# Zero-padded lo keys: both score products of a grouped head on 128 rows

## The chip, the core and the metric

The kernel runs on one core of a Trainium2 chip. Its engines are TensorE (PE, whose weight loads the profile lists as PEld), VectorE (DVE), ScalarE (ACT), GpSimd (POOL) and SyncE (SP, which issues most DMAs). Each engine works through its own list of instructions in order and waits on semaphores that the others raise. The metric is the device time of one execution in microseconds (us); lower is better.

## The reference

Two layers of a hybrid transformer trunk run over 128 context tokens and 512 latent tokens with shared weights. The part that matters here is the grouped-query attention of the latent tokens: 8 query heads of 64 channels share 2 key/value heads, and each latent query sees 640 keys (512 latent, 128 cached).

```python
def _gqa_attend(q, k, v):
    ...
    scale = HEAD_DIM ** -0.5

    def one(qblk):
        s = jnp.einsum('bqhgd,bkhd->bhgqk', qblk, k).astype(jnp.float32) * scale
        p = jax.nn.softmax(s, axis=-1).astype(v.dtype)
        return jnp.einsum('bhgqk,bkhd->bqhgd', p, v)
```

Beside it run a gated linear recurrence (RG-LRU) and a differential attention with 4 heads of two components of 32 channels. An output projection and a gated convolutional feed-forward network follow in each layer.

## The kernel before

All products are split for precision: a float32 value is the sum of a rounded hi part and a lo part (its remainder), and hi·hi, hi·lo and lo·hi are accumulated. The weights stream from DRAM, ACT rounds them (L329) and DVE subtracts (L330).

A layer has five stages: the input projections, during whose last part the context's attention runs; the attention of the latent tokens; the output projection; the two groups of the feed-forward network; residuals and norms in between. The order in which the instructions of one engine stand is written at build time. In the projections `Flow` writes side work when its due time has come. In the attention `Plan` places tasks by assumed lengths, keys and limited room (three pairs of PSUM banks `ps`, for example). A grouped score task is entered there with 540 ns.

**Queries.** For query head h of key/value head g the stationary tile `qa` has 128 rows: rows 64g to 64g+63 hold the hi part of the 64 channels, the other 64 rows the lo part (L828 to L848).

**Keys.** `k_stack` (L867) makes three transposes for 128 keys. Two go to `kk`, which has for each key/value head the hi part in both halves of the 128 rows. The third has the lo parts of both heads one above the other, and one ACT copy (L885) puts it into `kl`, a tile of 128 rows x 640 columns in the pool `tslots` (11 slots).

**Scores.** The unit G of the attention is one query head with one tile of 128 queries; there are 32 of them per layer. Its scores are 128 x 640 and lie in two PSUM banks of 320 columns. Each bank takes two products: `kk` against all 128 rows of `qa` (L1144), then `kl` against the 64 rows that hold the query's hi part (L1145):

```python
pe.matmul(s[:, b * 512:b * 512 + CH], lhsT=Q[:, qs], rhs=kk[:, ks], start=True, stop=False)
pe.matmul(s[:, b * 512:b * 512 + CH], lhsT=Q[hr, qs], rhs=kl[hr, ks], start=False, stop=True)
```

Then DVE takes the row maximum (L1155), ACT the exponential (L1159), which frees the pair of banks, DVE the reciprocal of the sum (L1164), POOL scales the probabilities (L1170), PE transposes them (L1179) into another pair of banks, ACT copies them out (L1184), and PE multiplies them with the values (L1202). The unit D of the differential heads (16 per layer) has two scores of one 96-row product per bank (L1149). PE also does 8 products per row block of the conditioning weights (L487, `ada`) between the units.

**The slots around it.** The pool `halves` has 22 slots of 128 rows x 1292 columns. Activations `hh` and `hl`, `cx` (the context's queries and keys), `kk`, the RG-LRU tiles and `mix` (the attention's input to the output projection) lie in it. A tile that takes over a slot waits for the last reader of the tile that was there. `mix_out` (L637) is the end of the RG-LRU: ACT copies the hi part (L639), DVE subtracts the lo part (L640).

Of the kernel before, what the change touches and what calls it, by code (L numbers as in the profile page):

```python
# [22 lines left out]
T = L + S  # L23
# [27 lines left out]
def f32(ap):  # L51
    return ap.bitcast(F32)


class Flow:
    """Order in which the program is written down. The tensor engine's products are the clock: after each block of
    them step() writes the side work that is due by then, as far as the vector engine's time allows."""
# [36 lines left out]
class Plan:  # L94
    """Order in which the attention is written down: tasks with an engine, a length, what they wait for and what they
    hold, started in the order of their keys as engines come free."""
# [49 lines left out]
def plan_attention(plan, par, ngen, unit, values, stack, ada, split, ready):  # L146
    """the tasks of a layer's attention: lengths in ns, what they wait for, and keys by the place of their unit"""
# [65 lines left out]
def hybrid_kernel(ctx: ExitStack, tc: tile.TileContext, i, o):  # L213
# [27 lines left out]
    def psum_mode(double, single):  # L241
        """the accumulators as so many pairs of banks and so many single banks"""
        psum.close()
        for key, n in (("ps", double), ("pb", single)):
            if n:
                mode[key] = psum.enter_context(tc.tile_pool(name=key, bufs=n, space=bass.MemoryType.PSUM))
# [9 lines left out]
    def pb2(name, cut=CH):  # L256
        """two banks for all tokens and where they are cut"""
        return [pb(name), pb(name), cut]
# [77 lines left out]
    def weights(ahead=2):  # L336
        """the next 128 rows x 1024 of weights in two float32r parts; the one after it is split now"""
        done = lambda: sum(isinstance(z, tuple) for z in split_done)
        while done() < ahead and pos[1] < len(parts) and len(split_done) - done() < 2:
            split_next()  # L340
        return split_done.pop(0)
# [9 lines left out]
    def pow_rstd(ss, n, mean):  # L351
        """(ss * mean + eps) ** -0.5 on [128, n]"""
        a = small("rs_a", n)
        r = small("rs_r", n)
        pool.tensor_scalar(out=a, in0=ss, scalar1=mean, scalar2=EPS, op0=ALU.mult, op1=ALU.add)
        pool.tensor_tensor(out=r, in0=a, in1=mhalf[:, 0:n], op=ALU.pow)
        return r

# [5 lines left out]
    # norm1_g and the bias of the first shift and scale, as rows  # L364
# [50 lines left out]
    def late_constants():  # L415
# [3 lines left out]
        # ffn convolution weights and biases as columns  # L419
# [14 lines left out]
        # differential-attention lambda, on every partition  # L434
# [6 lines left out]
        # softplus(-lambda) = max(-lambda, 0) + 2 atanh(z / (2 + z)), z = exp(-|lambda|), and the factors of log a  # L441
# [35 lines left out]
    res = {}  # L477

    def ada_gen(l, u):
        """one third of the modulation of a layer: a row block of its weights each time"""  # L480
        acc = pb("ada")
        for k in range(KD):
            while not split_done:
                split_next()
            n = split_done.pop(0)
            for j in range(4):
                pe.matmul(acc[32 * j:32 * j + 32, :], lhsT=cc[:, k].rearrange("p a b -> p (a b)"), rhs=raws[n][:, j, :],  # L487
                          start=(k == 0), stop=(k == KD - 1), tile_position=(0, 32 * j))
            load_to(n + 2)
            if k == KD - 2:  # L490
                bias, ar, src = tslot("abias", 512), tslot("arow", 512), i["ada_b"]
                sp.dma_start(out=bias, in_=bass.AP(tensor=src.tensor, offset=src.offset + l * 6 * D + u * 2048,
                                                   ap=[[512, 4], [0, 32], [1, 512]]))
            fl.now += 1100
            yield
        dve.tensor_tensor(out=ar, in0=acc, in1=bias, op=ALU.add)
        if u:
            d = drp.tile([2, 1024], F32, tag=f"gate{u}", name=f"gate{u}")
            for j in range(2):
                r = 32 * (j + (0 if u == 1 else 2))  # L500
                sp.dma_start(out=d[:, j * 512:(j + 1) * 512], in_=ar[r:r + 2, :])
            res["g", l, u] = d
        yield
        pt = pb("adaT")
        for b in range(4):
            pe.transpose(pt[:, b * 128:b * 128 + 128], ar[:, b * 128:b * 128 + 128], ident)
        c = smp.tile([128, 2, 4, 4], F32, tag=f"cm{u}", bufs=2, name=f"cm{u}")
        for r in range(2):
            dve.tensor_copy(out=c[:, r], in_=pt.rearrange("p (b j q) -> p q j b", b=4, j=4)[:, r])
        res["c", l, u] = c.rearrange("p r j b -> p r (j b)")  # L510
# [8 lines left out]
    def mod_cols(c_sh, c_sc, gain, name):  # L519
        """A = (1 + sc) * g, B = sh as columns [128, cond, 8]"""  # L520
        a = smp.tile([128, 2, KD], F32, tag=name, bufs=2, name=name)
        for r in range(2):
            dve.scalar_tensor_tensor(out=a[:, r], in0=c_sc[:, r], scalar=1.0, in1=gain, op0=ALU.add, op1=ALU.mult)
        return a, c_sh

# [12 lines left out]
    def norm_a(t):  # L538
        """a token tile by its rstd"""
        r = row_rstd(t)  # L540
        n = [tslot("xn", 512) for _ in range(2)]
        for hf in range(2):
            pool.tensor_scalar(out=n[hf], in0=x[:, t, hf * 512:hf * 512 + 512], scalar1=r, scalar2=0.0, op0=ALU.mult, op1=ALU.add)
        return n
# [46 lines left out]
    def stat_mm(acc, w, hh, hl, c, n0=0, n1=KD):  # L591
        """rows of weights stationary, one half of the tokens moving"""
# [9 lines left out]
    def tok_acc(name):  # L602
        """accumulators of 512 columns for the five token tiles"""
        box = {}

        def get(t):
            if t not in box:
                box[t] = pb(name)
            return box[t]
        return get  # L610

# [16 lines left out]
    def mixer(l, hh, hl, first=None):  # L628
# [119 lines left out]
        # stationary / moving stacks of the attention and what they come from  # L748
# [33 lines left out]
        def rope(src, t, tab, nh, hd):  # L782
            """src * cos + swapped(src) * sin on [128, nh * hd], in place"""
# [83 lines left out]
        def k_stack(kf, c0):  # L867
            """kf [128 tok, 2 heads of 64] float32 -> columns c0.. of kk (hi; hi) and of the lo of both heads"""
# [10 lines left out]
            def tr():  # L879
# [5 lines left out]
                act.activation(out=kkq[1][:, c0:c0 + 128], in_=f32(pt[:, 256:384]), func=ACTF.Copy)  # L885
# [6 lines left out]
        def d_stack(df, dest, c0, order, jp):  # L892
            """df [128 tok, 4 comps of 32] -> stacks of 96 rows, in columns c0.. of dest (two comps each): four steps"""
# [42 lines left out]
        def values():  # L936
            kkq.extend([v2(half("kk", F32R), T), tslot("kl", T, F32R)])
# [83 lines left out]
        def ctx_probs(qT, kT, kd):  # L1021
            """softmax numerators of 4 context score blocks and their sums; row tiles write to different banks"""
# [103 lines left out]
        dn, mixf, PTs = [], {}, {}  # L1126

        def unit(kind, h, q):
            """scores, softmax and transposed probabilities of one tile of queries of one head"""
# [4 lines left out]
            def score(c):  # L1134
# [3 lines left out]
                if kind == "G":  # L1138
                    kv = h // 4
                    Q, hr = qa[p][:, e], slice(64 * kv, 64 * kv + 64)  # L1140
                    kk, kl = kkq[0][:, kv], kkq[1]
                    for b in range(2):
                        ks = slice(b * CH, b * CH + CH)
                        pe.matmul(s[:, b * 512:b * 512 + CH], lhsT=Q[:, qs], rhs=kk[:, ks], start=True, stop=False)  # L1144
                        pe.matmul(s[:, b * 512:b * 512 + CH], lhsT=Q[hr, qs], rhs=kl[hr, ks], start=False, stop=True)  # L1145
# [43 lines left out]
        def values_of(kind, p, q):  # L1189
            """values of a pair of heads for one tile of queries, and of the context's with the last"""  # L1190
# [97 lines left out]
    def tok_products(nk, stat, done, last=4):  # L1288
        """one half of the columns: token tiles stationary, weights moving; the last row blocks go tile by tile"""
# [26 lines left out]
    def norm_pipe(t, AB, h):  # L1316
        """norm of token tile t as side work; transposes wait until their input is there"""
# [167 lines left out]
    # silu of the conditioning vectors as columns, replicated over 32 stationary columns  # L1485
# [158 lines left out]
```

## Time and profile before

| | |
|---|---|
| median of 3 runs | 1685.59 us (1685.24 to 1686.19) |
| span of the profiled execution | 1688.6 us; no time outside the span is given |
| PE busy | 1649.6 us, 98% of the span |
| DVE, ACT, POOL busy | 943.9, 725.1, 341.2 us (56%, 43%, 20%) |
| attention of the latent tokens, layer 0 and 1 | from 175.7 to 328 us and from 1004.7 to 1151 us of the span |

An engine's busy time counts its own instructions, and idle time before an instruction is put down to what ended it. PE's products are pipelined, so the time that a product costs is the distance between the starts of two products, not the duration in its row. [...]

### The profile page before, as it was taken

The numbers are of one execution on the slowest core, as the hardware profiler recorded it, in microseconds if no ns is written. First come the engines' busy times: TensorE is split into PE (matmuls) and PEld (weight loads), VectorE is DVE, ScalarE is ACT, GpSimd is POOL, SyncE is SP. The second block draws the span as 40 slices with busy tenths as digits, with TensorE's granted clock in tenths as the row PEclk, the third lists the DMA queues.
The fourth block names the chain that finished last, engine by engine and source line by source line (L and its number), as shares of the span: only waits on it lengthen the run. The fifth ranks groups of instructions, "written<-read, shape, count | busy, mean of one in ns | idle before, by whom it ended". The sixth has DMA issues, their size and how long they took to land. (4 is left out here: it accounts for less than half of the span.)

```text
span 1688.6 us, 25351 instructions
## 1 busy us (share of the span) xinstructions
PE 1649.6 (98%) x10070; PEld 1409.1 (83%) x10070; DVE 943.9 (56%) x1548; ACT 725.1 (43%) x1490; POOL 341.2 (20%) x742
## 2 busy tenths in 40 slices
PE   6999999999999999999999999999999999999998
PEld 4778666689999889999887776667899998899986
DVE  5787666466555334555377775665645553345544
ACT  4745566744333212333247455675433331133331
POOL 4162232213111000111053412320411110011101
PEclk9999799999999999999999998999999999999999
DMA  9222355521222321222212213343121322121212
GB/s 332 75 68 82 125 177 182 186 75 51 76 76 74 127 75 50 75 77 77 98 42 76 63 57 125 108 151 130 39 88 50 100 100 75 50 100 51 100 63 87
DMA packets 99434, 161.03 MB, mean 95 GB/s; under 512 B 10670, under 2 KB 69222, under 8 KB 94196
## 3 DMA queue, kind: packets, MB, share of 16 engines
q1 hardware_dynamic: 98068, 158.00, 27.7%
q8 instruction: 79, 1.29, 0.3%
q0 software_dynamic: 1040, 1.14, 0.2%
q14 instruction: 39, 0.32, 0.1%
q10 hardware_dynamic: 208, 0.28, 0.0%
HBM read 155.95 MB, written 3.44 MB: 94 GB/s over the span
## 5 line engine op out<-in xcount | busy, mean ns | idle before, releaser
L330 DVE TENSOR_TENSOR wl<-raw,wh 128x1024 fp32r<-128x1024 f32 x180 | 220.2, 1229 | 408.8 <-ACT wh L329 407.9
L345 PE MATMUL uacc<-hl,wh 128*128 128x320 f32 (+2 forms) x1408 | 436.1, 310 | 0.8 <-DVE hl L574 0.5
L344 PE MATMUL uacc<-hh,wh 128*128 128x320 f32 (+2 forms) x1408 | 436.6, 310 | 0.0
L346 PE MATMUL uacc<-hh,wl 128*128 128x320 f32 (+2 forms) x1408 | 436.4, 310 | 0.1
L329 ACT ACTIVATE wh<-raw 128x1024 fp32r<-128x1024 f32 x180 | 189.6, 1059 | 179.0 <-PE tacc L346 143.0
L345 PEld LDWEIGHTS uacc<-hl,wh 128*128 128x128 f32 x1408 | 265.0, 188 | 1.7 <-DVE hl L574 1.6
L346 PEld LDWEIGHTS uacc<-hh,wl 128*128 128x128 f32 x1408 | 265.7, 189 | 0.7 <-DVE wl L330 0.7
L344 PEld LDWEIGHTS uacc<-hh,wh 128*128 128x128 f32 x1408 | 264.8, 188 | 0.3
L344 PE MATMUL tacc<-wh,g 128*128 128x512 f32 x440 | 173.9, 395 | 0.0
L345 PE MATMUL tacc<-wl,g 128*128 128x512 f32 x440 | 173.5, 394 | 0.0
L346 PE MATMUL tacc<-wh,g 128*128 128x512 f32 x440 | 173.5, 394 | 0.0
L1155 DVE TENSOR_REDUCE nm<-S 128x1 f32<-128x640 f32 x128 | 104.0, 821 | 75.9 <-PE S L1145 53.7
L1159 ACT ACTIVATE P<-S,nm 128x640 f32<-128x640 f32 x128 | 101.3, 793 | 57.3 <-DVE nm L1155 46.6
L1362 POOL TENSOR_SCALAR ca<-u,fcol 128x642 f32<-128x642 f32 x44 | 39.1, 889 | 417.2 <-issue 244.0
L1170 POOL TENSOR_SCALAR P<-P,den 128x640 f32<-128x640 f32 x96 | 79.2, 828 | 216.7 <-DVE den L1164 130.5
L1358 ACT ACTIVATE u<-uacc 128x192 f32<-128x192 f32 (+1 forms) x88 | 29.1, 331 | 185.3 <-PE uacc L346 185.3
L346 PEld LDWEIGHTS tacc<-wh,g 128*128 128x128 f32 x440 | 82.6, 188 | 19.7
L345 PEld LDWEIGHTS tacc<-wl,g 128*128 128x128 f32 x440 | 82.7, 188 | 19.2
L344 PEld LDWEIGHTS tacc<-wh,g 128*128 128x128 f32 x440 | 82.6, 188 | 19.3
L344 PE MATMUL acc<-wh,hh 128*128 128x512 f32 x240 | 97.7, 407 | 0.0
L345 PE MATMUL acc<-wl,hh 128*128 128x512 f32 x240 | 95.9, 400 | 0.0
L346 PE MATMUL acc<-wh,hl 128*128 128x512 f32 x240 | 95.6, 398 | 0.0
(290 smaller groups left out, 2703.2 us busy)
## 6 DMA issues: line engine op xcount, KB each, us to landing
raw<-in_ffn_w_up_dram SPq DMA_DIRECT2D x44, 1024.0 KB, 4.9
raw<-in_ada_w_dram SPq DMA_DIRECT2D x40, 1024.0 KB, 4.9
raw<-in_ffn_w_down_dram SPq DMA_DIRECT2D x20, 1024.0 KB, 5.0
raw<-in_w_in_dram SPq DMA_DIRECT2D x16, 1024.0 KB, 8.6
araw<-in_ada_w_dram SPq DMA_DIRECT2D x16, 512.0 KB, 10.1
raw<-in_w_out_dram SPq DMA_DIRECT2D x8, 1024.0 KB, 5.0
gates<-gate SPq DMA_DIRECT2D x8, 512.0 KB
x<-in_x_sample_dram SPq DMA_DIRECT2D x4, 512.0 KB
```

The lines of the kernel that those rows point to most:

```text
L329: act.activation(out=wh, in_=raw, func=ACTF.Copy)
L330: dve.tensor_tensor(out=wl, in0=raw, in1=f32(wh), op=ALU.subtract)
L344: pe.matmul(out, lhsT=lh, rhs=rh, start=start, stop=False)
L345: pe.matmul(out, lhsT=lh, rhs=rl, start=False, stop=False)
L346: pe.matmul(out, lhsT=ll, rhs=rh, start=False, stop=stop)
L1155: dve.tensor_reduce(out=box["nm", c], in_=view(c), op=ALU.max, axis=AX.XY, negate=True)
L1159: act.activation(out=box["P"][c].rearrange("p (a b) -> p a b", a=2), in_=view(c), func=ACTF.Exp, bias=box["nm", c], accum_out=box["den"][: ...
L1170: pool.tensor_scalar(out=P[-1], in0=P[-1], scalar1=den[:, 1 + comps:2 + comps], scalar2=0.0, op0=ALU.mult, op1=ALU.add)
L1358: act.activation(out=u[:, 1 + cut:1 + L], in_=acc[1][:, 0:L - cut], func=ACTF.Copy)
L1362: pool.tensor_scalar(out=out, in0=u[:, 1:1 + n], scalar1=wcol(1), scalar2=wcol(3), op0=ALU.mult, op1=ALU.add)
```

## The change

The lo keys move from one 640-column tile in `tslots` to a tile in `halves` with one block of 640 columns for each key/value head. In the block of head g only rows 64g to 64g+63 hold lo keys; POOL sets the other 64 rows to zero once per layer (the tile is not written there again). The ACT copy of 128 rows becomes two copies of 64 rows. The second score product uses all 128 rows of `qa`, of which the lo rows now meet zeros. Apart from this only comments differ.

```diff
@@ k_stack
-                act.activation(out=kkq[1][:, c0:c0 + 128], in_=f32(pt[:, 256:384]), func=ACTF.Copy)
+                for g in range(2):
+                    gs = slice(64 * g, 64 * g + 64)
+                    act.activation(out=kkq[1][gs, g, c0:c0 + 128], in_=f32(pt[gs, 256:384]), func=ACTF.Copy)
@@ values
-            kkq.extend([v2(half("kk", F32R), T), tslot("kl", T, F32R)])
+            kkq.extend([v2(half("kk", F32R), T), v2(half("kl", F32R), T)])
+            for g in range(2):
+                pool.memset(f32(kkq[1][64 - 64 * g:128 - 64 * g, g]), 0.0)
@@ unit, score
-                    Q, hr = qa[p][:, e], slice(64 * kv, 64 * kv + 64)
-                    kk, kl = kkq[0][:, kv], kkq[1]
+                    Q, kk, kl = qa[p][:, e], kkq[0][:, kv], kkq[1][:, kv]
...
-                        pe.matmul(s[:, b * 512:b * 512 + CH], lhsT=Q[hr, qs], rhs=kl[hr, ks], start=False, stop=True)
+                        pe.matmul(s[:, b * 512:b * 512 + CH], lhsT=Q[:, qs], rhs=kl[:, ks], start=False, stop=True)
```

PE, DVE and SP keep their instructions in the same order. ACT has ten more (five per layer). Before, around the last key block of layer 0 (`cdk` and `cx` belong to the context, `kk` and `kl` are the keys):

```order
114 L1008 ACTIVATE cdk<-acc 128x256
115 L883 ACTIVATE kk<-kT 128x2x128
116 L885 ACTIVATE kl<-kT 128x128
117 L1016 ACTIVATE cx<-cdkT 128x256
118 L329 ACTIVATE wh<-raw 128x1024
```

The same place of ACT with the change:

```order
114 L1012 ACTIVATE cdk<-acc 128x256
115 L883 ACTIVATE kk<-kT 128x2x128
116 L887 ACTIVATE kl<-kT 64x128 x2
117 L1020 ACTIVATE cx<-cdkT 128x256
118 L329 ACTIVATE wh<-raw 128x1024
```

One copy has become two of half the rows, and nothing else has moved. POOL gets its two memsets between the sum of the RG-LRU's directions (`lruS`) and the norm of the first key tile (`rs_a`, `rs_r`), here in layer 0:

```order
60 L356 TENSOR_TENSOR rs_r<-rs_a,mhalf 128x8
61 L734 TENSOR_TENSOR lruS<-lruI 128x640
62 L941 MEMSET kl 64x640 x2
63 L355 TENSOR_SCALAR rs_a<-hss 128x2
64 L356 TENSOR_TENSOR rs_r<-rs_a,mhalf 128x2
```

Since `kl` takes a slot of `halves` and leaves one of `tslots`, later tiles of both pools land in other slots, and some of their first writers wait for another reader. The one such wait that was not already over in the trace of before is that of the ACT copy into the first `mix` tile of each layer (L639). In the built program of before, it waits in layer 0 for PE's 736th product, the last of the context's scores `cS` (L1030), and with the change for the 759th, the second L345 of the accumulator `lacc`'s last half.

## Rows read from the trace of the kernel before

**Rows 1.** Windows of both attentions: us, busy us (count) per engine, PEclk, DMA.

```profile
177.00:194.00 17.00, 17.00 (x57) 8.84 (x56) 7.62 (x18) 6.80 (x14) 5.55 (x9) 0.50 0.23 70
194.00:328.00 134.00, 133.31 (x1136) 88.06 (x1133) 84.02 (x179) 89.31 (x194) 38.90 (x51) 1.00 0.53 186
1006.40:1027.00 20.60, 20.60 (x64) 10.70 (x63) 9.69 (x22) 8.50 (x17) 6.75 (x11) 0.51 0.20 60
1027.00:1151.00 124.00, 122.83 (x1060) 84.87 (x1059) 80.92 (x172) 87.13 (x191) 36.26 (x49) 1.00 0.38 131
```

**Rows 2.** Costliest groups: busy us, mean ns | idle before, releaser.

```profile
L1155 DVE TENSOR_REDUCE nm<-S 128x1 f32<-128x640 f32 x128 | 104.0, 821 | 75.9 <-PE S L1145 53.7
```

**Rows 3.** Source view of L1145: count, ns min/median/max, starts, forms.

```profile
L1145 PE MATMUL S<-kl,qa x128: 407/410/633, 176.0 to 1141.9; 64*128 64x320 f32 x128
```

**Rows 4.** Windows of L1145 alone: us, PE busy (count), PEld, PEclk, DMA.

```profile
177.00:194.00 17.00, 5.38 (x9) 2.28 (x8) 0.50 0.23 70
1006.40:1027.00 20.60, 7.58 (x12) 3.42 (x12) 0.51 0.20 60
```

**Rows 5.** Timeline of PE, one grouped score: start us, us, instruction.

```profile
210.50 0.39 PE L1144 MATMUL S<-kk,qa 128*128 128x320 f32 x1
210.83 0.41 PE L1145 MATMUL S<-kl,qa 64*128 64x320 f32 x1
...
211.85 0.77 PE L1179 MATMUL PT<-ident,P 128*128 128x128 f32 x5
```

**Rows 6.** Timeline of PE, projection products of the same 320 columns.

```profile
166.08 0.31 PE L344 MATMUL lacc<-hh,wh 128*128 128x320 f32 x1
...
166.37 0.31 PE L346 MATMUL lacc<-hh,wl 128*128 128x320 f32 x1
```

**Rows 7.** Timeline of PE, a differential score and what follows.

```profile
243.91 0.54 PE L1149 MATMUL S<-dks,dqs 96*128 96x320 f32 x2
244.37 1.31 PE L1202 MATMUL PV<-PT,va 128*64 128x128 f32 x20
```

**Rows 8.** Timeline of PE, a grouped score at the half clock.

```profile
184.02 0.64 PE L1144 MATMUL S<-kk,qa 128*128 128x320 f32 x1
...
186.28 0.63 PE L1144 MATMUL S<-kk,qa 128*128 128x320 f32 x1
```

**Rows 9.** Timeline, a score, its exponential, and the next score but one.

```profile
246.02 0.31 PE L1144 MATMUL S<-kk,qa 128*128 128x320 f32 x1
...
248.67 0.79 ACT L1159 ACTIVATE P<-S,nm 128x640 f32<-128x640 f32 x1 [0.64 <-DVE den L1164]
...
250.44 0.39 PE L1144 MATMUL S<-kk,qa 128*128 128x320 f32 x1
```

**Rows 10.** Timeline before the attentions, the last row from layer 1; idle in brackets.

```profile
167.51 0.74 ACT L639 ACTIVATE mix<-lrug 128x640 fp32r<-128x640 f32 x1 [2.15 <-PE cS L1030]
168.43 0.81 DVE L640 TENSOR_TENSOR mix<-lrug,mix 128x640 fp32r<-128x640 f32 x1
169.83 0.48 DVE L903 TENSOR_TENSOR ds<-db,ds 128x128 fp32r<-128x128 f32 x2
170.28 0.32 PE L345 MATMUL lacc<-hl,wh 128*128 128x320 f32 x1
170.59 0.41 PE L908 MATMUL dT<-identr,ds 128*96 128x128 f32 x4
175.72 0.38 PE L1144 MATMUL S<-kk,qa 128*128 128x320 f32 x1 [0.69 <-DVE dks L912]
...
996.49 0.74 ACT L639 ACTIVATE mix<-lrug 128x640 fp32r<-128x640 f32 x1 [2.12 <-PE cS L1030]
```

**Rows 11.** Source view of L885, groups of L654, timeline of POOL.

```profile
L885 ACT ACTIVATE kl<-kT x10: 272/297/328, 142.5 to 985.4; 128x128 fp32r<-128x128 f32 x10
L654 POOL MEMSET lruW<- 128x512 f32 x4 | 2.1, 530 | 0.0
116.41 0.20 POOL L355 TENSOR_SCALAR rs_a<-hss 128x2 f32<-128x2 f32 x1 [5.49 <-DVE hss L801]
```

## The prediction

> **What bounds the kernel now.** I read the page first: PE is busy for 98% of the span, so the question is what PE's time consists of in the stage that changes. Next the windows of the two attentions [rows 1]: PE counts 133.31 of 134.00 us and 122.83 of 124.00 us, ACT 89.31 and 87.13, DVE 84.02 and 80.92. So PE sets the pace there and the next engine, ACT, has about a third of its time free. The groups say the same from the other side [rows 2]: the maximum of a score waits 53.7 us in all for the last score product L1145. Each attention begins with a stretch at half the clock, 17.0 us in layer 0 and 20.6 us in layer 1, and in it too PE counts busy throughout [rows 1].
>
> Then I looked at how long a score keeps PE, by the starts of its products. From the first of the four products of a grouped score to the next work it is 211.85 - 210.50 = 1.35 us [rows 5], 0.34 us for each. Products of the same 320 columns on 128 rows in the projection start (166.37 - 166.08) / 2 = 0.145 us apart [rows 6]. A differential score, two products of the same 320 columns on 96 rows, takes 244.37 - 243.91 = 0.46 us with its entry and its exit into another form [rows 7]. The duration of L1145 itself, 410 ns in the median [rows 3], is 0.1 us over the 0.31 of a 128-row product [rows 6]. So a grouped score pays a pause of about 0.2 us at each step from 128 to 64 rows and back, four steps per unit. At the half clock a unit takes 186.28 - 184.02 = 2.26 us [rows 8].
>
> **The score products.** With the change all four products have 128 rows. I take the entry and exit from the differential score and two plain steps in between: 0.46 + 2 x 0.145 = 0.75 us at most, and 4 x 0.145 = 0.58 at least where nothing changes form at either end; middle 0.67. Saving 1.35 - 0.67 = 0.68 us per unit at the full clock. There are 128 products L1145 [rows 3], 9 + 12 = 21 of them in the half-clock stretches [rows 4], so about 10 units there and 54 outside: 54 x 0.68 = 36.7 us. At the half clock I double the 0.67: 2.26 - 1.34 = 0.92, and 10 x 0.92 = 9.2 us. Together 45.9 us of PE time.
>
> **How much of it reaches the end.** PE has no idle time that would swallow it [rows 1], but it waits for its own results: three pairs of banks go round among scores and transposes, and a score may only start when the exponential three tiles back is done. One round from the rows: the score begun at 246.02 has its exponential from 248.67 to 249.46, and the score that takes its banks over starts at 250.44, so 0.98 us to spare [rows 9]. Two shortened scores lie between: 2 x 0.68 = 1.36 us earlier. If the exponential stays where it is, only 0.98 of 1.36 (72%) is gained; if it moves up with the scores, all of it. The sum of the work allows that: layer 0, with half of the 54 units, would have 134.0 - 27 x 0.68 = 115.6 us for ACT's 89.3 and DVE's 84.0 [rows 1]. But an engine at 77% queues more, and the conditioning weights must come some 14% faster, so I do not take the upper half for granted: 80%, between 60% (that round with a further wait in it) and 100%. 0.80 x 45.9 = 36.7 us, between 27.5 and 45.9.
>
> **The new slot of kl.** The copy into the first `mix` tile now waits for PE's 759th product. In the rows of before that is the L345 that starts at 170.28 and ends at 170.60, and the copy stood at 167.51 [rows 10]: 3.1 us later. ACT's queue behind it holds the context's exponentials. DVE's L640 waits for the copy (168.43, just behind its end at 168.25) and would start at 171.4, 3.0 us later. Everything on DVE behind L640 moves with it: the subtractions L903 at 169.83 go to 172.8, the first result is there 0.3 us later, and the transposes L908, which PE had at 170.59, need it. PE therefore stands from 170.6 to about 173.25: 2.7 us. The rest of the projection follows PE in its order, and I find no second wait that absorbs it, so the first score moves from 175.72 to 178.4. Layer 1 has the same rows (996.49) [rows 10]. Cost 2 x 2.7 = 5.4 us, all on PE's path. Bounds: 0, if ACT or DVE gets ahead of PE by another route, and twice that, 10.8, if the standstill takes the clock down for the 18 products of 0.145 us that follow (2.6 us more per layer).
>
> **The rest.** Ten more copies on ACT: the nearest row is the copy of 128 rows at 297 ns [rows 11]; two of 64 rows take between that in all and twice that, so 0 to 0.3 us for each key block, behind products that PE does not wait for; at nothing, and 3.0 us at most if every one were on the path. The memsets of 640 columns are a little over the 530 ns of a 512-column one, some 1.3 us per layer; POOL stands idle 5.49 us at that place [rows 11], and the norm behind them is not later. If that cover were gone it would be 2.6 us. One slot less among `halves` and one more among `tslots` moves other waits too, but all of them were over in the trace of before.
>
> **The sum.** -36.7 + 5.4 = -31.3 us. It is made against the profiled execution, whose span of 1688.6 us is 3.0 us (0.2%) over the median of the runs; I take the difference off the median: 1685.6 - 31.3 = 1654.3, say 1654 us.
>
> [...] The trace shows the 64-row product 0.1 us longer than the 128-row one and its successor 0.2 us later [rows 3, 5, 6]. [...]
>
> **Rivals.**
> - *The loop or another engine takes over (B).* If the round of banks, ACT or the weights' DMA becomes the bound, half is kept: 0.5 x 45.9 - 5.4 = 17.6 us, 1668 us. For it: only 0.98 us to spare in that round [rows 9]. Against it: a third of ACT and DVE is free [rows 1].
> - *The clock comes back early (C).* The half-clock stretches last 37.6 us [rows 1]; the scores in them were about 10.5 x 2.26 = 23.7, so 13.9 us were other work. With denser scores the clock may rise soon: 7.0 us off the other work and 10 x 0.67 = 6.7 off the scores, 80% of 13.7 is 11.0 us more: 31.3 + 11.0 = 42.3, 1643 us. For it: the clock stayed low while PE counted busy with paused products [rows 1, 8]. Against it: PE stands still longer just before, and the first units wait for their exponentials in any case. [...]
> - *The pause stays (D).* If it belongs to loading the same queries twice or to two products on one bank, the scores stay at 1.35 us and the wait at `mix` decides as soon as less than 5.4 us is saved: 1685.6 + 5.4 = 1691 us, slower. Against it: in the differential score both products use the same queries, in the projection three follow on one bank, without the pause [rows 6, 7].
>
> **How the numbers follow.** Forecast 0.52, B 0.20, C 0.22, D 0.06. The forecast's own bounds run from 27.5 - 5.4 = 22.1 (1664) to 45.9 - 5.4 = 40.5 (1645). For 8 in 10 the range takes in most of C and about half of B: 1640 to 1668. This kernel's measurement can tell 0.2% (3.4 us) from no change. Faster by more: all but D and a sliver of B, 0.93; within it 0.02; slower 0.05.
>
> **What would show it.** Right: four L1144 and L1148 products about 0.15 us apart, L1148 with a duration near 310 ns, attentions shorter by 15 to 20 us each, PE still the fullest engine there with some idle time before scores and transposes put down to ACT's exponentials. The slot's cost would show as idle time of some 2.5 us before a dT product (L910) shortly ahead of the first score, and as `mix` waiting for `lacc`. Wrong: products still 0.34 us apart (D), attention idle time of PE above 10 us per layer (B), or half-clock stretches under 10 us (C).

## The result and the profile after

The changed kernel takes 1641.44 us (median of 4 runs, 1637.77 to 1643.37); the kernel before took 1685.87 us beside it. The ratio is 0.9737, with a 95% interval from 0.9715 to 0.976: 44.4 us less. The prediction was 1654 us with a range from 1640 to 1668. The profiled execution has a span of 1641.6 us, with a mean granted clock of 0.995 (before: 1688.6 us and 0.986).

The same view of the windows as [rows 1], now of the changed kernel: the first 17 us of each attention, and the rest of it up to the output projection.

```profile
180.00:197.00 17.00, 16.25 (x145) 11.23 (x145) 13.30 (x33) 12.58 (x26) 6.50 (x10) 1.00 0.55 186
197.00:306.00 109.00, 107.74 (x1049) 78.61 (x1047) 78.87 (x167) 83.24 (x183) 38.33 (x49) 1.00 0.61 211
985.00:1002.00 17.00, 15.81 (x129) 11.88 (x131) 14.48 (x34) 13.95 (x27) 7.87 (x12) 1.00 0.39 129
1002.00:1103.00 101.00, 99.76 (x1000) 76.40 (x996) 76.35 (x164) 81.46 (x181) 35.33 (x47) 1.00 0.44 152
```

Two things differ from [rows 1]. The first 17 us now run at the full clock (PEclk, the granted clock as a share of full speed, is 1.00) and hold 145 and 129 PE instructions, where 17.0 us of before held 57 at the half clock (0.50). And PE is still full: it is not busy for 0.75 + 1.26 + 1.19 + 1.24 = 4.4 us of both attentions, after 1.9 us in [rows 1]. So hardly any of the time that was saved turned into waiting. From its first score product to the first product of the output projection layer 0 took 175.72 to 328.68 before and 179.81 to 306.18 now, 26.6 us less; layer 1 took 146.0 and now 118.0 us, 28.0 less. The prediction had named 15 to 20 us each. Its signs of B (over 10 us of idle time per layer) and D (products still 0.34 us apart) are absent; that of C (half-clock stretches under 10 us) is there. The stages outside lost 4.1 us ahead of the first score, 2.7 between the attentions and 0.8 behind the second.

The timeline of PE in the changed kernel shows two grouped scores in a row; its start column answers to [rows 5].

```profile
223.66 0.42 PE L1147 MATMUL S<-kk,qa 128*128 128x320 f32 x1
223.91 0.31 PE L1148 MATMUL S<-kl,qa 128*128 128x320 f32 x1
224.06 0.31 PE L1147 MATMUL S<-kk,qa 128*128 128x320 f32 x1
224.20 0.31 PE L1148 MATMUL S<-kl,qa 128*128 128x320 f32 x1
224.35 0.31 PE L1147 MATMUL S<-kk,qa 128*128 128x320 f32 x1
```

After the first step of 0.25 us the products start about 0.145 us apart, and the next unit begins 0.69 us after this one. It was 1.35 us [rows 5]. The source view of the lo products (answering to [rows 3]) and the group of the maximum (to [rows 2]) say it for all units:

```profile
L1148 PE MATMUL S<-kl,qa x128: 302/309/317, 180.0 to 1094.2; 128*128 128x320 f32 x128
```

```profile
L1158 DVE TENSOR_REDUCE nm<-S 128x1 f32<-128x640 f32 x128 | 102.9, 819 | 31.8 <-PE S L1152 16.8
```

The product's median goes from 410 to 309 ns, and the maximum's idle time from 75.9 to 31.8 us; its largest part is no longer put down to the lo product, but to the differential score.

The wait that the change adds stands in the timeline ahead of the first attention (compare [rows 10]; idle time in brackets):

```profile
170.75 0.74 ACT L639 ACTIVATE mix<-lrug 128x640 fp32r<-128x640 f32 x1 [4.49 <-PE lacc L345]
171.52 0.83 DVE L640 TENSOR_TENSOR mix<-lrug,mix 128x640 fp32r<-128x640 f32 x1 [2.69 <-ACT mix L639]
172.93 0.48 DVE L905 TENSOR_TENSOR ds<-db,ds 128x128 fp32r<-128x128 f32 x2
173.35 0.63 PE L910 MATMUL dT<-identr,ds 128*96 128x128 f32 x4 [2.49 <-DVE ds L905]
179.81 0.38 PE L1147 MATMUL S<-kk,qa 128*128 128x320 f32 x1 [0.70 <-DVE dks L914]
```

It is the predicted chain, link by link: ACT waits for the projection product, DVE for ACT, PE for DVE, 2.49 us. The first score comes 4.1 us later, not 2.7. The windows of that place show the rest:

```profile
170.60:173.20 2.60, 0.26 (x2) 0.00 (x0) 1.68 (x5) 2.42 (x5) 0.00 (x0) 1.00 0.01 3
173.20:176.60 3.40, 3.25 (x15) 3.28 (x16) 2.39 (x9) 3.11 (x10) 0.00 (x0) 0.50 0.00 0
```

PE stands almost still for 2.6 us, and then has a stretch of 3.4 us at the half clock, in which products of 320 columns start some 0.27 us apart. Layer 1 has the same (2.49 us of idle time, then 979 to 982 at 0.50). So the half-clock stretches of 17.0 and 20.6 us inside the attentions are gone, and two of 3.4 us ahead of them are new.

### The profile page after: what moved, and what is told of

Same layout as the page of the kernel before. It is cut to its first block, busy times and chain, and to the rows that moved or that the text cites. A ratio compares the mean times of both kernels' runs of the same rounds, so it can differ in the third digit from the quotient of the medians.

```text
span 1641.6 us, 25381 instructions
## 1 busy us (share of the span) xinstructions
PE 1594.2 (97%) x10070; PEld 1393.8 (85%) x10070; DVE 945.0 (58%) x1548; ACT 726.3 (44%) x1500; POOL 344.8 (21%) x746
## 5 line engine op out<-in xcount | busy, mean ns | idle before, releaser
L345 PE MATMUL uacc<-hl,wh 128*128 128x320 f32 (+2 forms) x1408 | 437.4, 311 | 0.8 <-DVE hl L574 0.5
L345 PEld LDWEIGHTS uacc<-hl,wh 128*128 128x128 f32 x1408 | 264.5, 188 | 1.7 <-DVE hl L574 1.6
L345 PE MATMUL tacc<-wl,g 128*128 128x512 f32 x440 | 173.8, 395 | 0.0
L1158 DVE TENSOR_REDUCE nm<-S 128x1 f32<-128x640 f32 x128 | 102.9, 819 | 31.8 <-PE S L1152 16.8
L345 PEld LDWEIGHTS tacc<-wl,g 128*128 128x128 f32 x440 | 82.7, 188 | 19.1
L345 PE MATMUL acc<-wl,hh 128*128 128x512 f32 x240 | 95.9, 399 | 0.0
```

The lines of the kernel that those rows point to most:

```text
L345: pe.matmul(out, lhsT=lh, rhs=rl, start=False, stop=False)
L1158: dve.tensor_reduce(out=box["nm", c], in_=view(c), op=ALU.max, axis=AX.XY, negate=True)
```

## The experiments

Three questions were open: what the pause belongs to, what holds the clock down at an attention's start, and what the slot costs. Each ratio is taken to runs of the kernel before on the same chip: 1686.5 us for the first four kernels, 1685.2 for the last three, which ran on another chip.

**s_slot: the slot's wait, with the pauses.** The changed kernel, with

```
+   hr = slice(64 * kv, 64 * kv + 64)
-   pe.matmul(..., lhsT=Q[:, qs], rhs=kl[:, ks], ...)
+   pe.matmul(..., lhsT=Q[hr, qs], rhs=kl[hr, ks], ...)
```

> The changed kernel's two tiles for the lo keys, with the products that use them cut back to the 64 rows that hold numbers: the slot's wait alone, with the paused products. Theory (the paused products themselves hold the clock down at an attention's start): the pauses are back, products 0.34 us apart, the wait costs 2.5 us of TensorE per layer and a half-clock stretch over 15 us long stands in each attention as before; time 1691 us (1688 to 1696) against 1685.6 before. Rival (the clock was low because of what lies ahead of the attention, which the wait changes): no half-clock stretch over 4 us, and a time under 1683 us.

Measured 1693.8 us (1683.9 to 1694.2; ratio to before 1.0049, 1.0033 to 1.0066): slower than before, as the theory had it. Its windows, of an execution that took 1683.9 us:

```profile
172.30:175.60 3.30, 3.30 (x16) 3.23 (x16) 2.12 (x7) 2.41 (x6) 0.00 (x0) 0.50 0.00 0
175.70:182.50 6.80, 5.90 (x30) 3.75 (x28) 4.92 (x10) 3.33 (x5) 0.00 (x0) 1.00 0.00 0
182.50:192.70 10.20, 10.20 (x35) 4.24 (x34) 4.84 (x13) 4.26 (x11) 3.68 (x6) 0.50 0.30 103
1008.50:1012.00 3.50, 3.50 (x15) 1.16 (x15) 1.54 (x4) 1.97 (x6) 1.17 (x2) 0.51 0.04 5
```

The clock had come back at 175.7, and it fell again at 182.5, in the paused scores, with PE counted busy throughout (10.20 of 10.20 us). This execution had only these 10.2 us of it in layer 0, and in layer 1 only some 3.4 us (last row), so the expected 15 us in each layer were missed here. The other four executions took 1689.7 to 1694.2 us at a mean clock of 0.986 to 0.990 instead of 0.994: they had more half-clock time. So paused scores at an attention's start do not bring a long stretch in every execution; what decides its length stays open.

**s_pairs: half as many changes of rows.** The kernel before, with both hi products ahead of both lo products:

```
    for b in range(2): pe.matmul(..., rhs=kk[:, ks], start=True, stop=False)
    for b in range(2): pe.matmul(..., rhs=kl[hr, ks], start=False, stop=True)
```

> The kernel before with the order of a unit's four score products changed to both hi products, then both lo products: the same products, two changes between 128 and 64 rows instead of four. Theory (the pause belongs to each change of the number of rows): the two products in the middle of each pair start 0.15 us apart, the pause goes from 4 x 0.34 = 1.35 to about 2 x 0.34 + 2 x 0.15 = 0.98 us per unit, 64 x 0.37 = 24 us of TensorE; time 1662 us (1655 to 1672). Rival (each product on 64 rows pays for itself): unit as before, 1685 us (1682 to 1689).

Measured 1653.5 us (ratio 0.9805, 0.978 to 0.983), 1.5 us under the lower end. One unit in its timeline:

```profile
208.86 0.56 PE L1144 MATMUL S<-kk,qa 128*128 128x320 f32 x2
209.35 0.56 PE L1147 MATMUL S<-kl,qa 64*128 64x320 f32 x2
209.84 1.06 PE L487 MATMUL ada<-raw,cc 128*32 128x512 f32 x8
```

A unit takes 209.84 - 208.86 = 0.98 us, the size that was expected. The products inside a pair start 0.24 us apart and not 0.15, though: a change of rows lengthens the step to the changed product and the step behind it. The lo products are still all on 64 rows, so the rival is out. The steps account for 64 x (1.35 - 0.98) = 23.7 of the 33 us. The rest may be the clock's, which was not separated here. The profiled execution has no half-clock stretch in the attention of layer 0 and one of 17.0 us in layer 1, with half the changes of rows:

```profile
175.60:193.00 17.40, 17.40 (x143) 11.03 (x143) 13.22 (x31) 12.01 (x25) 6.49 (x10) 1.00 0.55 182
985.20:1002.20 17.00, 17.00 (x63) 9.89 (x63) 9.42 (x22) 8.60 (x17) 7.09 (x11) 0.50 0.26 76
```

**s_all64: 64 rows without a change.** The changed kernel with `Q`, `kk` and `kl` all cut to `hr`.

> The changed kernel with all four score products of a unit on 64 rows; it leaves out the half of each hi product that belongs to the other 64 rows. Theory (the pause belongs to the change of the number of rows): no change, no pause, products 0.15 us apart, L1148 near 310 ns; time 1641 us (1637 to 1646). Rival (a product on 64 rows is slow by itself): products 0.34 us apart, four per unit, time over 1680 us.

Measured 1647.2 us (ratio 0.9778, 0.9761 to 0.9796), 1.2 us over the upper end. One unit:

```profile
211.17 0.41 PE L1148 MATMUL S<-kk,qa 64*128 64x320 f32 x1
211.42 0.31 PE L1149 MATMUL S<-kl,qa 64*128 64x320 f32 x1
211.56 0.30 PE L1148 MATMUL S<-kk,qa 64*128 64x320 f32 x1
211.71 0.30 PE L1149 MATMUL S<-kl,qa 64*128 64x320 f32 x1
211.95 1.06 PE L487 MATMUL ada<-raw,cc 128*32 128x512 f32 x8
```

Four products on 64 rows start as close as four on 128 rows. Only the way in (0.25) and out (0.24) are long, 0.78 us for the unit; 64 x (0.78 - 0.69) = 5.8 us is about what this kernel misses the expected 1641 by. The pause belongs to the change of rows, not to the 64 rows.

**s_own: a slot for `mix`.** One more tile in the pool, so that the first `mix` tile goes where it went in the kernel before:

```
-   hpool = ... tc.tile_pool(name="halves", bufs=22)
+   hpool = ... tc.tile_pool(name="halves", bufs=23)
-   tp = ... tc.tile_pool(name="tslots", bufs=11)
+   tp = ... tc.tile_pool(name="tslots", bufs=10)
-   ident = const.tile([128, 128], F32, name="ident")
+   ident = f32(identr)
```

(The lines that make `identr` ahead of this, from a temporary tile of `tslots`, are left out here.)

> The changed kernel with a 23rd tile in the pool that the lo keys come from (paid by one 2.6 KB slot that the changed kernel no longer uses and by one identity matrix kept once instead of twice), so that the first mixed tile takes the slot it took in the kernel before and waits for no product. Theory: the 2.5 us of TensorE's idle time ahead of a dT product and the 3.4 us at half clock behind it go in both layers, the first score product comes 4 us earlier; 1633 us (1630 to 1637) against 1641 for the changed kernel. Rival (the start of the attention would then wait for something else, the chain from the projection's end): under 2 us in all, 1640 us (1638 to 1643).

Measured 1631.7 us (1630.4 to 1631.9; ratio 0.9678, 0.9664 to 0.9692): faster than both kernels. The same place in its timeline:

```profile
167.41 0.74 ACT L641 ACTIVATE mix<-lrug 128x640 fp32r<-128x640 f32 x1 [1.78 <-PE cS L1036]
169.73 0.48 DVE L907 TENSOR_TENSOR ds<-db,ds 128x128 fp32r<-128x128 f32 x2
170.50 0.42 PE L912 MATMUL dT<-identr,ds 128*96 128x128 f32 x4
175.64 0.39 PE L1149 MATMUL S<-kk,qa 128*128 128x320 f32 x1 [0.69 <-DVE dks L916]
```

ACT copies at 167.41 again, PE has no idle time ahead of the transposes, and the first score is back at 175.64. No half-clock stretch is left near either attention: 175.6 to 300 us run at 1.00, all 128 products L1150 take 309 ns in the mean as in the changed kernel, and the 288 products of `lacc` ahead of the attentions 90.9 us as in the kernel before (90.8; 94.5 in the changed one).

**t_first, t_rest, t_both: which pauses hold the clock.** s_own with the lo products of some units on 64 rows, by a count of the units of each layer:

```
+   hr = slice(64 * kv, 64 * kv + 64) if len(gcount) < 6 else slice(0, 128)
+   gcount.append(h)
```

(`>= 6` in t_rest, always in t_both. The lo product then takes `Q[hr, qs]` and `kl[hr, ks]`.)

> The kernel of s_own (1631.7 us) with the lo products of only the first 6 of the 32 grouped units of each layer on 64 rows: 12 of 64 units get their pauses back, at an attention's start. A paused unit is 1.50 us from the product ahead of it to the product behind it and an unpaused one 0.82, so the pauses alone are 12 x 0.67 = 8 us. Theory (paused products at an attention's start hold TensorE at half clock): stretches of 14 to 20 us at half clock at the start of both attentions, as in the kernel before, worth 12 to 17 us more; time 1655 us (1648 to 1661), granted clock near 0.988. Rival (the clock doesn't hang on the pauses): no half-clock stretch over 4 us there, 1640 us (1636 to 1644).

> The kernel of s_own with the lo products of all but the first 6 grouped units of each layer on 64 rows: 52 of 64 units get their pauses back, none at an attention's start. Theory: no half-clock stretch over 4 us at an attention's start, granted clock 0.996 or more, and nearly all of 52 x 0.67 = 35 us comes back; time 1665 us (1659 to 1670). Rival A (pauses anywhere take the clock down): granted clock under 0.992, over 1672 us. Rival B (a good part of a pause is hidden by what TensorE waits for otherwise, as the prediction had it with 80%): 1659 us or less.

> The kernel of s_own with the lo products of all grouped units on 64 rows: all 64 pauses, without the slot's wait, so the kernel before but for the 23rd tile, the copies and memsets. Theory: half-clock stretches of 14 to 20 us at the start of both attentions in most executions, 1686 us (1681 to 1690) as the kernel before; the sum of what t_first and t_rest add over s_own. Rival (the pool's 23rd tile or the one identity matrix is what made s_own 10 us faster than the changed kernel): 1678 us or less.

Measured: t_first 1644.2 us (1642.1 to 1647.9), t_rest 1665.8 us (1663.7 to 1666.6), t_both 1683.5 us (1678.0 to 1686.9; ratio to before 0.9986, 0.9973 to 0.9999). Windows of the attentions' starts, t_first, t_rest (with the rest of each attention) and t_both in this order:

```profile
178.60:188.80 10.20, 10.20 (x35) 4.23 (x34) 4.82 (x13) 4.25 (x11) 3.65 (x6) 0.50 0.31 103
984.10:997.80 13.70, 13.70 (x46) 6.69 (x45) 6.76 (x17) 6.06 (x14) 4.74 (x7) 0.50 0.21 77
```

```profile
175.70:194.00 18.30, 17.55 (x156) 12.49 (x156) 14.33 (x35) 13.30 (x28) 7.54 (x12) 1.00 0.55 179
194.00:318.50 124.50, 123.35 (x1038) 80.86 (x1036) 78.41 (x166) 83.71 (x182) 36.69 (x48) 1.00 0.53 184
992.00:1010.00 18.00, 16.80 (x113) 11.31 (x113) 13.66 (x32) 13.72 (x26) 7.87 (x12) 1.00 0.36 118
1010.00:1126.70 116.70, 115.61 (x1013) 80.03 (x1011) 77.20 (x164) 81.76 (x182) 34.98 (x47) 1.00 0.39 132
```

```profile
177.10:194.10 17.00, 17.00 (x55) 8.80 (x56) 7.62 (x18) 6.84 (x14) 5.40 (x9) 0.50 0.23 69
1006.60:1023.60 17.00, 17.00 (x59) 9.10 (x58) 6.87 (x19) 6.85 (x17) 7.23 (x11) 0.50 0.26 81
```

Six paused units at the start bring the half clock back, for 10.2 and 13.7 us (a little shorter than expected); 26 paused units behind an unpaused start do not. The program ahead of the attention is the same in these kernels, and PE idles 0.69 us ahead of the first score in t_first as in s_own, so the paused scores at its start do it, and not the idle time ahead of them. The mean granted clocks agree: 0.988 to 0.992 in all four executions of t_first, 0.997 to 0.998 in s_own. In time t_first missed: 1644.2 us is under the theory's 1648 and just over the rival's upper end of 1644; it is the clock that decides against the rival. What the half clock costs was over-estimated: t_first is 12.6 us above s_own, of which 12 x 0.66 = 7.9 are pauses, so some 4.6 us are left for it and not 12 to 17. (The profiled executions have spans of 1644.5 us and, in s_own, 1629.9: 14.6 us more, 6.7 of them beyond the pauses.) t_rest came out as the theory had it: 34.2 us over s_own for 52 units, 0.66 us each, no half-clock stretch at an attention's start, granted clock 0.996 to 0.998. t_both came out within its range, and so did its half-clock stretches of 17.0 us. That it would be the sum of the other two was missed: 12.6 + 34.2 = 46.8 us over s_own, measured 51.8. It has 34.0 us at half clock at the attentions' starts and t_first 23.9, which fits a part of the difference. t_both is within 2 us of the kernel before, so the pool's 23rd tile and the single identity matrix are not what makes s_own faster.

## Why the prediction was right, and where its sizes were off

The runs give the four corners that the account needs. Without the slot's wait: 1631.7 us without pauses (s_own), 1683.5 with all of them (t_both). With the wait: 1641.4 us (the changed kernel) and 1693.8 (s_slot). The pauses are worth 51.8 us one way and 52.4 the other; the wait costs 9.8 and 10.4. The two parts add up. The kernels did not all run on one chip: each taken against its own runs of the kernel before, the pauses are worth 53.1 and 51.8 us and the wait 10.4 and 9.0, so these sizes are good to some 1.5 us.

**Score products: right.** A unit was to go from 1.35 to 0.67 us, and the rows show 0.69. The cause was named correctly: the change between 64 and 128 rows (s_pairs, s_all64). A unit takes 1.35 us with four changes, 0.98 with two and 0.69 with none. Products on 64 rows alone start about 0.145 us apart, as on 128 rows (s_all64). So the pause goes with the change from one product to the next, and not with a product on 64 rows by itself.

**How much reaches the end: the step that was mis-sized.** I kept 80% of the saving, since a round of score banks had only 0.98 us to spare [rows 9]. t_rest gives 0.66 us on the path for each paused unit, against 0.68 us of PE time by the forecast and 1.35 - 0.69 = 0.66 by the rows: 97% or more. The round had no wait of its own: the maximum waited for the scores (75.9 us in [rows 2], 53.7 of them for the lo product, and now 31.8), so it and the exponential moved up with them. That ACT at 77% would queue more was an estimate, and no run shows it: in the second window of the changed kernel ACT is busy for 83.24 of 109.00 us (76%), and PE idles 1.26 us. The alternative was in the prediction ("if it moves up with the scores, all of it"), and the sum of ACT's and DVE's work spoke for it. In the changed kernel this view of L1147 names what still stands in the way of the hi products (idle time of PE's weight loads, us and times):

```profile
  ACT P L1162: 7.2, 11
```

7.2 us over 11 of 128 products, much of it behind a running product: PE as a whole idles 4.4 us in both attentions.

**The clock: rival C came true, beside the forecast.** I gave it 0.22, with 11.0 us more. The 64 pauses at 0.66 us are 42.2 us; t_both over s_own is 51.8, so 9.6 us are the clock's, by difference. The forecast's own sum had 10 x (0.92 - 0.68) = 2.4 us of that, 1.9 at 80%. What I held against C, that the first units wait for their exponentials in any case, did not keep the clock low: the new windows have 0.75 and 1.19 us of idle time in the first 17 us, and run at 1.00. The rows of before could not tell whether idle time ahead or paused products keep the clock low at an attention's start; t_first shows that the paused products do. That C's 1643 us came within 2 us is in part luck: it had 36.7 + 11.0 = 47.7 us for pauses and clock where 51.8 were measured, and 5.4 for the slot where 9.8 were, and the two errors cancel.

**The slot: place and chain right, price too low.** 5.4 us was forecast, the idle time alone. That part is as predicted (2.49 against 2.7 us per layer). The stretch of 3.4 us at half clock behind it was only in the upper bound, 10.8. It does not follow every time: behind two such waits (5.4 us of PE's idle time in all in the changed kernel and s_all64, 5.5 in s_slot) it stands in both layers of the profiled changed kernel, where the 288 products of `lacc` with 320 columns take 94.5 us, but in one layer only of s_slot (layer 0) and of s_all64, where they take 92.7, half-way to the 90.9 of s_own. Against s_own the first score is 4.2 us late in layer 0 and another 4.1 in layer 1, 8.3 in all. The other 1.5 to 2.1 us of the 9.8 and 10.4 I can place only in part. The profiled execution of the changed kernel has a further stretch of 3.4 us at half clock from 920.5 on: eight products of 512 columns start 0.43 us apart in it and 0.23 behind it, 1.6 us in all. In s_own the 720 products `acc` of that form show none (285.3 us against 289.0), but its 48 products of `lacc` with 384 columns take 18.4 us against 16.5, the size of one such stretch. The four executions of the changed kernel differ too: the two at a mean granted clock of 0.998 took 1637.8 and 1639.7 us, 6.1 and 8.0 above s_own, the two at 0.995 took 1643.2 and 1643.4. So where the clock stays up, the price is not far from the 5.4 of the forecast. Which execution has such a stretch where stays open.

**The rest: right.** Twenty copies of 64 rows at 271 ns and four memsets at 627 ns are in t_both as well, and it is no slower than before (1.7 us less, barely clear of noise).

Sum of the measured parts: -42.2 - 9.6 - 1.7 + 9.8 = -43.7, measured -44.4. That they agree is no check, since the terms are differences along one chain of runs; the 0.7 between them is that of the two medians of the kernel before. The prediction's -31.3 came out 13 us short: 15.1 for pauses and clock (51.8 against 36.7; 7.4 of them the share, 7.7 the clock) and 1.7 for the rest, less 4.4 for the slot. The measured 44.4 us also lie beyond the best case of the forecast's own sum, 40.5 us or 1645 us. What held the time was the lower end of 1640, put there for C, and by 1.4 us: that is luck beside a mechanism that was right.

## What to carry to other kernels

An engine that counts busy all the time can still be full of pauses (here 133.31 of 134.00 us busy, with 0.34 us from start to start of products that start 0.145 us apart elsewhere): measure the distance between the starts of equal products, and compare it with that of the same product in another stage. Products on 64 rows among products on 128 should stand in groups (0.98 us a unit in s_pairs, not 1.35) or be padded to the same number; here zeros in the other 64 rows cost nothing on TensorE (about 0.145 us from start to start on 64 rows and on 128). When a change takes a slot from a pool, look at who gets a slot from a later release than before: giving the slot back was worth another 9.8 us.

## What the runs showed of the hardware

- A change of rows costs about 0.17 us in the kernel before ((1.35 - 0.69) / 4), and it is spread over the step to the changed product and the step behind it: with two products of each kind all steps are about 0.24 us, not 0.15 and 0.34 in turn (s_pairs).
- TensorE stayed at a granted clock of 0.50 for 17.0 us in which it counted busy for 17.00 us, with 55 to 59 instructions in them (t_both). The unpaused start of the changed kernel ran at 1.00 with 0.75 us of idle time in 17.0 us. Six paused units at an attention's start were followed by 10.2 and 13.7 us at 0.50 (t_first); 26 of them behind an unpaused start left both attentions at 1.00 (t_rest). The length is not fixed: paused starts had 17.0 us (t_both), but 10.2 and 3.4 in the profiled s_slot.
- 23.9 us at half clock in t_first cost some 6.7 us by the spans of the profiled executions, over a quarter of their length, and 4.6 us by the medians; both are what is left of the difference to s_own when the pauses are taken off.
- An idle time of 2.49 us of TensorE was followed by 3.4 us at 0.50 in both layers of the profiled changed kernel. In s_slot and s_all64 two such waits brought one such stretch each, by the sums of `lacc` (92.7 us against 94.5 and, in s_own without the wait, 90.9).
